# A mixer's softmax: probabilities scaled by 1/z on GpSimd ahead of their transposes, nine low parts of weights formed by GpSimd, and a new order

## The chip, the cores and the metric

The kernel runs on one core of a Trainium2 chip. The metric is the device time of one execution in microseconds (us), taken as the median of a few runs. Lower is better.

## What is computed

One layer of an encoder, on x of 512 positions by 1024 channels, all in float32:

```python
x = x + 0.5 * swiglu(rms_norm(x, ffn1_norm), ...)          # D_FF = 2752
u = rms_norm(x, mix_norm) @ w_in                           # 512 | 8x64 q | 2x64 k | 2x64 v
f_out = fourier_mixer(u[..., :512], fnet_w, fnet_b)        # Re(FFT2) per group of 128, then a linear map
a_out = gqa_attention(q, k, v, q_norm, k_norm)             # 8 query heads, 2 key heads, 512 x 512 scores
    p = jax.nn.softmax(scores, axis=-1); o = p @ v
x = x + concat([f_out, a_out]) @ w_out
x = x + 0.5 * swiglu(rms_norm(x, ffn2_norm), ...)
y = rms_norm(x, final_norm)
```

The change is in the attention of the middle part, in how the division by the softmax's sum z is done.

## The kernel before

**Numbers in two parts.** Every matrix operand is kept as a high part, rounded to the type fp32r that TensorE multiplies quickly, and a low part, the rest. A product takes three matmuls (high x high, high x low, low x high; `product`, L179). The high part of a weight is a cast, mostly on ACT; the low part is a subtraction, `lows` (L126), on VectorE.

**Stages.** First the feed-forward part (`ffn`, 0 to 330.9 us of the span), then the mixer (330.9 to 486.6), then the second feed-forward part with the final norm. The mixer works on 512 positions in eight banks of PSUM.

**The mixer's order.** Each step of the mixer is a named function in `ops`. The string `ORDER` (L47) lists all names; they are emitted in that order (L1314), and each of the five engines (PE, DVE, Activation, Pool, SP) then runs its own instructions strictly in the order of emission. Banks, buffers and slots are given out in that order too. So an instruction that waits on an engine holds up everything behind it on that engine.

**The names.** In names of the form `s`t`b`c, t is one of four pairs of query heads, b one of two key heads, c a block of 128 positions.

- `wX.r`, `wX.h`, `wX.l` (L799 to L817), and the same for `f0` to `f3`, `fw`, `o0` to `o7`: load a weight by a DMA from SP's queue into one of three `raw` buffers, cast its high part (ACT; VectorE for `f0` and `f1`), form its low part (VectorE). The two parts take a pair of slots out of three pairs in the mixer, so a high part waits until TensorE is through with the weight three back. A raw buffer is free when the low part is done.
- `k.0` to `k.7`, `q0.0` ..., `v.0` ...: the projections, one product each (L825). `.sq`, `.sw`, `.sd`, `.rc`, `.rs`, `.pq`, `.s0`, `.s1` (L838 to L900): squares, swapped halves by four small DMAs on SP's queue (`.sd`), rotation, and the norm of a head, whose power of -1/2 is on GpSimd (`.s1`, L900; `n1.p` is another, L255). `.ah`, `.al`, `.bh`, `.bl`: the parts of q.
- `f00.0` ... (L1003): Fourier projections; `map0`, `d00` ..., `c0.c` ...: the rest of the Fourier mixer. `pos` (L1310): three DMAs of its tables, issued by GpSimd.
- `s` (L1139): scores, two matmuls into a bank. `m` (L1146): on VectorE the maximum over a row (L1148) and a multiplication of 128x1 by the row's scale (L1149). `e` (L1152): the exponential on ACT, which also sums each row into `zs[t]`. The result, `prob[t, b, c]`, has queries on partitions and keys along them.
- `t` (L1164): four transposes of `prob` by TensorE, so that keys lie on partitions; each needs all four c of its t and b. `h` and `l` (L1171, L1177): high and low part of the transposed probabilities. `v` (L1206): values times probabilities, into `outs[t, b]`. `o..c`, `o..a` (L1218 to L1227) add the two halves of it into `pair[t]`.
- `z0.r`, `z0.w`, `z0.p` (L1186 to L1200): 1/z of all eight columns of a pair on VectorE, spread over 64 columns each by GpSimd, and turned into a row by four transposes on TensorE, into a bank. `r0.m` (L1231): the row multiplied into `pair[t]` on VectorE. `r0.h`, `r0.l`: its parts for the output projection.
- `y0.0` ... `y7.7` (L1242): the output projection; `.x`, `.h`, `.l`, `.q`, `.a`: residual, norm operands and squares.

So before, probabilities are left unscaled up to the very end, and 1/z is multiplied in once for each pair of heads.

Of the kernel before, what the change touches and what calls it, by code (L numbers as in the profile page):

```python
# [41 lines left out]
HI_DVE = ("f0", "f1")  # L42
SWAP_DMA = ("q1", "q2", "q3")
# [4 lines left out]
wq0.r wk.r wv.r wk.h pos wq0.h wk.l k.0 k.1 k.2 k.3 wq1.r k.4 wq1.h k.5 k.6 k.7 wv.h n1.c k.sq wq0.l q0.0  # L48
q0.1 q0.2 cos k.pq wq1.l n1.m q0.3 q0.4 k.sw f3.r q0.5 wv.l wq2.r k.s0 q0.6 k.s1 k.rc q0.7 q1.0 wq2.h k.rs
q1.1 q1.2 q1.3 q0.rc q0.sq kw f1.r wq2.l kp v.0 q0.sw km k0.2 q0.pq k0.0 k1.0 q0.s0 v.1 q1.4 q0.rs k1.3 q1.5  # L50
v.2 wq3.r k0.1 v.3 q0.bh q1.6 k0.3 q1.7 q2.0 q0.ah q1.sq q0.al s000 v.4 q0.bl v.5 wq3.h s001 s002 s003 q0.s1
v.6 k1.1 m000 k1.2 q1.sw wq3.l q1.sd q2.1 e000 m002 m003 q1.rc m001 q1.pq e002 v.7 q1.s0 q1.rs vt q3.0 s011
q1.s1 e001 q2.2 m011 vp q2.3 q1.ah q2.4 s010 f0.r f2.r q1.al q3.1 q2.5 q2.6 e003 q2.7 f0.h q3.2 n1.p m010
q2.sw s012 q3.3 f0.l f1.h t000 e010 q2.sd e011 q2.rc m012 t003 vs q2.sq h000 fw.r t001 s013 e012 s102 t002
f1.l m102 q3.4 v.h q3.5 h002 q3.6 f00.0 l000 s100 m013 h001 l002 v.l l001 e013 e102 q3.7 q2.pq f2.h m100 v000
q3.sw z0.r q3.sd t010 q2.s0 q1.bh q2.s1 v001 q2.rs f01.0 e100 f2.l s101 f00.1 q2.ah h010 m101 q3.sq f02.0
q1.bl l010 o2.r s103 v002 e101 f02.1 h003 t011 q3.rc q2.bh f00.u l003 h011 m103 q2.bl v003 t013 f02.e e103
t012 o0.r q3.rs q3.pq s112 v010 q3.ah l011 f01.1 q2.al s110 q3.s0 h012 h013 s113 l012 v011 o00.c o00.a l013
m113 m112 s212 e113 m110 f03.0 f01.u e112 m212 q3.al o1.r t103 f03.1 f3.h t101 h101 v012 q3.s1 h103 f03.e
l101 v013 e212 t100 h100 o01.c f10.0 f3.l l103 fw.h s213 l100 q3.bh f12.0 o01.a s111 f03.h f10.1 f02.h q3.bl  # L60
t102 f10.u f03.l e110 s210 s211 h102 v100 m213 z0.w e213 f02.l m111 v101 e111 s201 m210 m211 f12.1 o5.r l102
f12.e e211 z0.p r0.m t111 t112 v102 h111 h112 fw.l l112 v103 o10.c s203 f12.h e210 t110 f11.0 h110 m201 l111
o4.r m203 f13.0 o10.a t113 o0.h s202 t210 f12.l e203 l110 f11.1 v110 r0.h o0.l h113 s200 f11.u m202 f13.1
r0.l z1.r e201 map1 l113 t211 m200 v111 o1.h map1.h map0 f13.e d00 d01 h210 f13.h o1.l map1.l f13.l l210
map0.h v112 v113 e200 t213 d0.h h211 map0.l l211 s302 e202 s301 v210 t212 h213 h212 d0.l d10 z1.w m302 o11.c
d11 v211 e302 l213 t200 s300 d1.h l212 m301 d1.l h200 o11.a t201 c0.s v212 s311 m300 c0.c e301 m311 c0.q t203
e300 e311 h203 d20 v213 o21.c s303 d21 c0.o h201 l200 t202 v200 o3.r m303 s312 l203 c1.c z2.r e303 o21.a c1.s
d30 c0.h d2.h l201 c1.q z1.p t300 m312 v201 d2.l c1.o d31 c2.s h202 e312 r1.m s310 l202 s313 c2.q c1.h t301
d3.h c0.l m313 c2.c h300 v202 e313 c1.l v203 y0.0 o20.c m310 h301 l300 c2.o y0.1 e310 d3.l l301 o20.a z2.w
z3.r y1.0 y1.1 c2.h t303 v300 o2.h c3.s c3.c t310 v301 c3.q o7.r t302 c2.l y1.2 h310 h303 c3.o h302 y0.2 l302  # L70
t312 z2.p c3.h v302 c3.l t311 h311 l310 l303 y1.3 y1.4 o6.r z3.w r1.h l311 t313 v310 y0.3 h313 o2.l v303
o30.c r1.l y2.0 y1.5 v311 y2.1 h312 l313 l312 r2.m v312 v313 z3.p o30.a y2.2 y0.4 r2.h o31.c r2.l o31.a y1.6
y0.5 r3.m y0.6 r3.h y2.3 r3.l y0.7 y2.4 o3.h y2.5 y2.6 o3.l y1.7 y2.7 y1.x y3.0 o5.h o5.l y3.1 y3.2 y2.x y0.x
y3.3 y2.q o4.h y5.0 y3.4 o4.l y3.5 y5.1 y0.q y1.q y3.6 y5.2 y5.3 y3.7 y5.4 y5.5 y4.0 y5.6 y4.1 y3.x y4.2 o6.h
y1.h y4.3 y2.h y5.7 y4.4 o6.l y4.5 o7.h y5.x y0.h y6.0 y5.h y4.6 y3.h y1.l y1.a o7.l y3.q y6.1 y2.l y5.q y4.7
y7.0 y4.x y4.q y3.l y7.1 y6.2 y2.a y7.2 y4.h y6.3 y5.l y6.4 y6.5 y3.a y0.l y7.3 y6.6 y6.7 y4.a y5.a y7.4 y6.x
y4.l y7.5 y6.h y6.l y6.q y7.6 y7.7 y7.x y6.a y7.q y7.h y7.a y7.l
# [3 lines left out]
def asf(ap):  # L81
    return ap.bitcast(F32)
# [3 lines left out]
def encoder(ctx, tc, A, out):  # L86
# [39 lines left out]
    def lows(lo, src, hi):  # L126
        nc.vector.tensor_tensor(out=lo, in0=src, in1=asf(hi), op=ALU.subtract)  # L127
# [619 lines left out]
    with tc.tile_pool(name="mix", bufs=1) as mp, tc.tile_pool(name="mixt", bufs=1) as mt:  # L747
# [51 lines left out]
        def weight_ops(name, src, n=KD):  # L799
# [14 lines left out]
            @op(f"{name}.l")  # L814
            def _():
                hi, lo = ws[name]
                lows(lo[:, :n, :], raws[name][:, :n, :], hi[:, :n, :])  # L817
# [314 lines left out]
        prob, parts, pts, outs, pair, zs, zps, sps, mxs = {}, {}, {}, {}, {}, {}, {}, {}, {}  # L1132
# [50 lines left out]
        def sum_ops(t):  # L1183


            @op(f"z{t}.r")  # L1186
            def _():
                nc.vector.reciprocal(zs[t], zs[t])

            @op(f"z{t}.w")  # L1190
            def _():
                zw = tp.tile([P, 4, 2, HD], F32, tag="wide", bufs=1, name=f"zw{t}")
                nc.gpsimd.tensor_copy(zw, zs[t].unsqueeze(3).to_broadcast([P, 4, 2, HD]))
                zs[t] = zw
# [353 lines left out]
```

## Time and profile before

| | us |
|---|---|
| median of three runs | 826.18 |
| the three runs | 824.57, 826.18, 826.47 |
| span of the profiled execution, first to last instruction | 821.1 |
| the mixer within it | 330.9 to 486.6 |
| median less span | 5.1 |

The profile is of one execution, which is shown by its span; the median is of other executions and holds also what lies around the span. Granted clock of TensorE: 1.000. In the rows of the profile, PE is TensorE's matmuls, PEld its loads of the stationary operand, DVE VectorE, ACT ScalarE, POOL GpSimd, SP the queue that issues most DMAs. A row of a group gives line, engine, operation, out<-in with shapes, count, busy us, mean ns of one, and the engine's idle time just before; a row of the timeline begins with start and length in us. `mix` is any of the mixer's banks in PSUM. Matmuls overlap, so their length is more than the distance from one start to the next.

### The profile page before, as it was taken

Reading aid. Unit: us, or ns where it says so; the run is one execution under the profiler, and the core shown is the slowest. Engines: PE = TensorE matmul, PEld = TensorE weight load, DVE = VectorE, ACT = ScalarE, POOL = GpSimd, SP = SyncE. Lnnn points to the kernel's source line nnn. Section 1 sums busy time; section 2 is a strip of 40 time slices with the busy share of each in tenths; the row PEclk is TensorE's granted clock in tenths of the full one; section 3 lists DMA queues with packets and bytes.
Section 4 is the critical chain, followed back from the end, with each engine's and each line's share of the span. In section 5 each row is a group of like instructions: output and inputs, shape, how many; then the busy total and the mean of one; then the engine's idle time right before and its main releaser. Section 6 shows DMA issues by size and latency. Waiting matters only on the chain.

```text
span 821.1 us, 13621 instructions
## 1 busy us (share of the span) xinstructions
PE 814.0 (99%) x5378; PEld 747.0 (91%) x5378; DVE 640.8 (78%) x996; ACT 464.5 (57%) x777; POOL 30.6 (4%) x34
## 2 busy tenths in 40 slices
PE   9999999999999999999999999999999999999997
PEld 7889999899989998889998888899989999899986
DVE  7998896489756947799998488998945896479574
ACT  7764664167524635676886358556632673256462
POOL 0110000000000000222000000100000000000001
PEclk9999999999999999999999999999999999999999
DMA  7664322323242213621110233552232322322222
GB/s 257 182 145 174 123 91 78 123 103 141 66 153 89 74 58 116 225 77 52 52 52 27 87 105 105 123 170 112 93 121 112 126 103 69 131 104 97 69 78 103
DMA packets 31168, 89.58 MB, mean 109 GB/s; under 512 B 3712, under 2 KB 8832, under 8 KB 31104
## 3 DMA queue, kind: packets, MB, share of 16 engines
q1 hardware_dynamic: 27776, 82.61, 28.9%
q0 software_dynamic: 2608, 5.12, 3.3%
q10 hardware_dynamic: 720, 0.98, 0.3%
q8 instruction: 42, 0.69, 0.3%
q14 instruction: 22, 0.18, 0.1%
HBM read 84.24 MB, written 2.10 MB: 105 GB/s over the span
## 4 chain that ended last, share of the span: by engine, by line
PE 97%; DVE 1%; issue 1%; DMA 0%; ACT 0%; POOLq 0%; POOL 0%; DVEq 0%
PE dn L183 25%; PE r L419 23%; PE q L419 12%; PE mix L183 9%; PE gu L183 8%; PE p L419 6%; PE gu L708 3%; PE mix L1211 2%; PE mix L1168 2%; PE mix L1142 1%; PE mix L1006 1%; PE mix L1008 1%; PE mix L1007 1%; PE mix L1143 1%; PE mix L1065 1%
## 5 line engine op out<-in xcount | busy, mean ns | idle before, releaser
L419 PE MATMUL r<-rt,ring 128*128 128x256 f32 x1686 | 209.3, 276 | 0.0
L183 PE MATMUL dn<-at,ring 128*128 128x512 f32 x900 | 203.3, 380 | 0.5 <-DVE ring L127 0.4
L419 PEld LDWEIGHTS r<-rt,ring 128*128 128x128 f32 x1686 | 200.4, 188 | 0.8
L183 PEld LDWEIGHTS dn<-at,ring 128*128 128x128 f32 x900 | 168.1, 188 | 29.8 <-DVE ring L127 1.6
L419 PE MATMUL q<-rt,ring 128*128 128x256 f32 x840 | 106.6, 276 | 0.0
L127 DVE TENSOR_TENSOR ring<-s,ring 128x1024 fp32r<-128x1024 f32 x70 | 85.6, 1223 | 24.0 <-ACT ring L378 20.8
L419 PEld LDWEIGHTS q<-rt,ring 128*128 128x128 f32 x840 | 100.4, 188 | 0.0
L543 DVE SCALAR_TENSOR_TENSOR gx<-dn,gx 128x512 f32<-128x512 f32 x61 | 42.0, 690 | 67.6 <-PE dn L183 67.6
L378 ACT CAST ring<-s 128x1024 fp32r<-128x1024 f32 x70 | 73.5, 1050 | 28.0 <-PE p L419 13.6
L169 ACT CAST ring<-raw_dn 128x768 fp32r<-128x768 f32 (+3 forms) x58 | 45.2, 783 | 71.1 <-PE dn L183 62.2
L127 DVE TENSOR_TENSOR ring<-raw_dn,ring 128x768 fp32r<-128x768 f32 (+3 forms) x58 | 51.6, 893 | 5.7 <-PE r L419 4.4
L419 PE MATMUL p<-rt,ring 128*128 128x256 f32 x420 | 53.3, 276 | 0.0
L127 DVE TENSOR_TENSOR ring<-raw_g,ring 128x1024 fp32r<-128x1024 f32 x35 | 42.8, 1221 | 11.1 <-PE p L419 10.2
L419 PEld LDWEIGHTS p<-rt,ring 128*128 128x128 f32 x420 | 50.2, 188 | 0.0
L183 PE MATMUL gu<-ring 128*128 128x512 f32 x216 | 48.9, 381 | 0.0
L183 PEld LDWEIGHTS gu<-ring 128*128 128x128 f32 x216 | 40.4, 188 | 6.9
L378 ACT CAST ring<-raw_g 128x1024 fp32r<-128x1024 f32 x35 | 36.8, 1051 | 15.8 <-DMA raw_g<-in_wgu 8.5
L427 ACT COPY p<-r 128x256 f32<-128x256 f32 x35 | 13.0, 371 | 46.8 <-PE r L419 46.5
L451 ACT ACTIVATE g<-g 128x512 f32<-128x512 f32 x35 | 22.1, 633 | 23.4 <-DVE g L450 23.1
L387 ACT CAST ring<-raw_u 128x512 fp32r<-128x512 f32 x35 | 21.8, 624 | 17.4 <-PE q L419 15.9
L183 PE MATMUL mix<-near,ring 128*128 128x512 f32 x120 | 29.7, 383 | 0.0
L464 DVE TENSOR_TENSOR u<-g,u 128x512 f32<-128x512 f32 x35 | 24.1, 689 | 6.1 <-ACT u L463 6.0
(269 smaller groups left out, 1300.5 us busy)
## 6 DMA issues: line engine op xcount, KB each, us to landing
raw_g<-in_wgu SPq DMA_DIRECT2D x35, 512.0 KB, 3.6
raw_u<-in_wgu SPq DMA_DIRECT2D x35, 512.0 KB, 4.4
raw_dn<-in_wd SPq DMA_DIRECT2D x40, 384.0 KB, 3.1
raw_gu<-in_wgu SPq DMA_DIRECT2D x12, 512.0 KB, 3.7
raw_o<-in_wo SPq DMA_DIRECT2D x8, 512.0 KB, 3.5
raw_dn<-in_wd SPq DMA_DIRECT2D x8, 448.0 KB, 3.4
raw_wq<-in_wins SPq DMA_DIRECT2D x4, 512.0 KB, 3.6
raw_f<-in_winf SPq DMA_DIRECT2D x4, 512.0 KB, 4.5
```

What stands on the lines that cost most here:

```text
L127: nc.vector.tensor_tensor(out=lo, in0=src, in1=asf(hi), op=ALU.subtract)
L169: nc.scalar.copy(hi[:, :n, :], raw[:, :n, :])
L183: nc.tensor.matmul(ps, a, b, start=first and b is mhi and a is whi, stop=last and a is wlo)
L378: nc.scalar.copy(hi, src)
L387: nc.scalar.copy(hi, src)
L419: nc.tensor.matmul(ps[:, t], a[:, ks], b[:, i, t], start=first and i == 0 and o == 0, stop=i == KH - 1 and o == 2, skip_group_check=not first,
L451: nc.scalar.activation(b["g"], b["g"], AF.Silu)
L464: nc.vector.tensor_tensor(out=u, in0=b["g"], in1=u, op=ALU.mult)
L543: nc.vector.scalar_tensor_tensor(out=x[d][:, t], in0=ps[:, t], scalar=0.5, in1=x[d][:, t], op0=ALU.mult, op1=ALU.add)
L708: nc.tensor.matmul(turned(pss[c]), w[:, k % 2, c], turned(m[k]), start=k == 0 and m is hh and w is hi, stop=k == KD - 1 and w is lo,)
L1168: nc.tensor.transpose(pts[n][:, c * P : (c + 1) * P], prob[t, b, c][:, kc * P : (kc + 1) * P], ident)
L1211: nc.tensor.matmul(turned(outs[t, b]), w, turned(p), start=kc == 0 and i == 0, stop=kc == 3 and i == 1)
```

## The change

- `z{t}.r`, `.w`, `.p` and `r{t}.m` go: no spread copy, no sixteen transposes, no four multiplications, and the bank for the row goes with them.
- `z{t}{b}` takes the reciprocal of one half of `zs[t]` (eight of them, where there were four of the whole).
- `p{t}{b}{c}` multiplies each of the 32 tiles of probabilities by its column of 1/z, in place, on GpSimd, between `e` and `t`.
- The low parts of `wq1`, `wq2`, `wq3`, `wv`, `f0` to `f3` and `fw` are formed by GpSimd; `wk`, `wq0` and `o0` to `o7` stay on VectorE.
- `ORDER` is new throughout: all five engines run their mixer steps in another order. Only its beginning, and a piece with the first head's `z` and `p`, are shown.

```diff
+LOWS_POOL = ('wq1', 'wq2', 'wq3', 'wv', 'f0', 'f1', 'f2', 'f3', 'fw')
...
-wq0.r wk.r wv.r wk.h pos wq0.h wk.l k.0 k.1 k.2 k.3 wq1.r k.4 wq1.h k.5 k.6 k.7 wv.h n1.c k.sq wq0.l q0.0
...
+wk.r wk.h wk.l wq1.r wq0.r k.0 k.1 k.2 k.3 k.4 wv.r k.5 wq0.h k.6 n1.c cos wq0.l q0.0 q0.1 k.7 wq1.h wv.h q0.2
+q0.3 wq3.r k.sq q0.4 q0.5 n1.m k.pq wq1.l k.s0 q0.6 wv.l q0.7 v.0 v.1 q1.0 q1.1 q1.2 k.sw wq2.r k.rc q0.sw k.s1
...
+vt s011 q1.ah q2.sq f0.h q1.pq q1.s0 s012 m003 q2.sw q3.1 q3.2 n1.p s013 m011 e010 e000 q3.3 q1.al e003 f0.l
+m013 q1.s1 q1.bh vp f1.h z00 e013 q3.4 m012 s101 q1.bl f2.r e011 q2.pq q3.5 p000 f00.0 m101 p001 vs s103 o2.r
+p002 m103 q2.rc e012 q2.sd q3.6 q3.7 z01 p003 f1.l q2.rs e101 f3.r t002 v.h q3.sq q3.sw q2.s0 t003 p010 f2.h
...
-    def lows(lo, src, hi):
-        nc.vector.tensor_tensor(out=lo, in0=src, in1=asf(hi), op=ALU.subtract)
+    def lows(lo, src, hi, by=nc.vector):
+        by.tensor_tensor(out=lo, in0=src, in1=asf(hi), op=ALU.subtract)
...
-                lows(lo[:, :n, :], raws[name][:, :n, :], hi[:, :n, :])
+                lows(lo[:, :n, :], raws[name][:, :n, :], hi[:, :n, :], nc.gpsimd if name in LOWS_POOL else nc.vector)
...
-            @op(f"z{t}.r")
-            def _():
-                nc.vector.reciprocal(zs[t], zs[t])
-
-            @op(f"z{t}.w")
-            def _():
-                zw = tp.tile([P, 4, 2, HD], F32, tag="wide", bufs=1, name=f"zw{t}")
-                nc.gpsimd.tensor_copy(zw, zs[t].unsqueeze(3).to_broadcast([P, 4, 2, HD]))
-                zs[t] = zw
-
-            @op(f"z{t}.p")
-            def _():
-                zps[t] = bank_for(f"z{t}")
+            for b in range(2):
+
+                @op(f"z{t}{b}")
+                def _(b=b):
+                    nc.vector.reciprocal(zs[t][:, :, b], zs[t][:, :, b])
+
                 for c in range(4):
-                    nc.tensor.transpose(zps[t][:, c * P : (c + 1) * P], zs[t][:, c].rearrange("p a b -> p (a b)"), ident)
+
+                    @op(f"p{t}{b}{c}")
+                    def _(b=b, c=c):
+                        e = prob[t, b, c]
+                        nc.gpsimd.tensor_scalar(out=e, in0=e, scalar1=zs[t][:, c, b : b + 1], scalar2=None, op0=ALU.mult)
...
-            @op(f"r{t}.m")
-            def _():
-                nc.vector.tensor_tensor(out=pair[t], in0=zps[t], in1=pair[t], op=ALU.mult)
-                read(f"z{t}")
-
```

More of the change, by code (lines that the diff above doesn't have):

```diff
@@ L47 @@
 ORDER = """
-wq0.r wk.r wv.r wk.h pos wq0.h wk.l k.0 k.1 k.2 k.3 wq1.r k.4 wq1.h k.5 k.6 k.7 wv.h n1.c k.sq wq0.l q0.0
[L49 to L62, printed above, removed]
@@ L68 @@
[L68 to L72, printed above, removed]
```

37 lines of the change are left out of this document (26 added, 11 removed).

## The prediction

> **What bounds the kernel now.** I read the page first, for the engine that ends the span, then the stretch of the mixer in five windows, then the waits inside it, then the chain. The first two lines are the page's head, the third its chain of work.
>
> ```profile
> span 821.1 us, 13621 instructions
> PE 814.0 (99%) x5378; PEld 747.0 (91%) x5378; DVE 640.8 (78%) x996; ACT 464.5 (57%) x777; POOL 30.6 (4%) x34
> ...
> PE 97%; DVE 1%; issue 1%; DMA 0%; ACT 0%; POOLq 0%; POOL 0%; DVEq 0%
> ```
>
> The chain is 97% TensorE, so only TensorE's own work or an idle gap on it can change the time. The mixer is the stretch from 330.9 to 486.6. Columns: stretch, then busy us of PE, PEld, DVE, ACT, POOL.
>
> ```profile
> 360.00:390.00 30.00, 30.00 (x200) 27.22 (x198) 28.87 (x53) 19.60 (x40) 7.03 (x5) 1.00 0.20 63
> 390.00:420.00 30.00, 30.00 (x216) 27.81 (x215) 28.96 (x56) 25.68 (x53) 0.62 (x1) 1.00 0.19 71
> 420.00:452.00 32.00, 32.00 (x203) 28.53 (x201) 28.64 (x60) 23.33 (x48) 1.23 (x2) 1.00 0.06 18
> 452.00:486.60 34.60, 34.60 (x159) 29.53 (x158) 22.14 (x29) 15.80 (x23) 0.00 (x0) 1.00 0.28 92
> ```
>
> TensorE is busy in all of it, at granted clock 1.00. VectorE is a close second: 86.5 of the 92 us from 360 to 452, so 5.5 us spare. GpSimd is nearly empty. A busy PE may hide waits, so I looked for TensorE among the waits of this stretch; there is one row:
>
> ```profile
> PEld mix L1142 <- DVE near L127: 0.4, 1, 0.4
> ```
>
> To see that no more is hidden, I added up TensorE's work by its spacings (start to start). Rows, the last from the chain:
>
> ```profile
> 379.63 0.38 PE L1142 MATMUL mix<-ks,near 128*128 128x512 f32 x1
> ...
> 380.08 0.38 PE L1211 MATMUL mix<-ph,near 128*128 128x512 f32 x1
> ...
> 380.52 0.28 PE L1006 MATMUL mix<-ring 128*128 128x256 f32 x1
> ...
> 381.91 0.60 PE L1168 MATMUL mix<-ident,e 128*128 128x128 f32 x4
> ...
> 415.44 0.87 PE L1065 MATMUL mix<-pos,near 128*128 128x258 f32 x6
> 416.16 0.62 PE L1065 MATMUL mix<-both,near 128*128 128x512 f32 x2
> ...
> 417.08 0.39 PE L1211 MATMUL mix<-ph,near 128*128 128x512 f32 x1
> ...
> 431.00 0.60 PE L1200 MATMUL mix<-ident,zw 128*128 128x128 f32 x4
> 431.43 0.60 PE L1168 MATMUL mix<-ident,e 128*128 128x128 f32 x4
> 431.79 0.47 PE L1211 MATMUL mix<-ph,near 128*128 128x512 f32 x1
> 432.10 0.38 PE L1211 MATMUL mix<-pl,near 128*128 128x512 f32 x1
> ```
>
> ```profile
> 452.22 34.37 PE mix L183 x156
> ```
>
> A score (s) or attended (v) step takes 0.445 us, half a Fourier projection (f) 1.38, the two halves of d 0.72 and 0.92, a product of three matmuls 3 x 34.37/156 = 0.66, a map step about as much, a c step a quarter of an f. Four transposes take 0.36 and make what follows 0.08 late: 431.79 to 432.10 is 0.31 where a plain matmul of 512 takes 0.22. Laid end to end from 330.92 in the old order, these make 485.5; the chain's products end at 452.22 + 34.37 = 486.6. So about 1.1 us in 156 is spacing that I can't name, and the floor of this stretch is TensorE's own work. Nothing taken off VectorE shortens the kernel by itself.
>
> **The change, part by part.** Rows by group (count, busy us, mean ns):
>
> ```profile
> L1200 PE MATMUL mix<-ident,zw 128*128 128x128 f32 x16 | 2.4, 272 | 0.0
> ...
> L1193 POOL COPY zw<-z 128x512 f32<-128x512 f32 x4 | 2.5, 613 | 54.0 <-PE mix L1200 30.8 <-ACT fu L1018 23.2
> ...
> L1232 DVE TENSOR_TENSOR oo<-mix,oo 128x512 f32<-128x512 f32 x4 | 2.7, 684 | 0.1
> ...
> L1188 DVE RECIPROCAL z<-z 128x8 f32<-128x8 f32 x4 | 0.8, 192 | 0.0
> ...
> L127 DVE TENSOR_TENSOR ring<-raw_f,ring 128x1024 fp32r<-128x1024 f32 x3 | 3.7, 1218 | 0.0
> ...
> L1334 POOL TENSOR_TENSOR gx<-gx,rb 128x256 f32<-128x256 f32 x2 | 1.4, 733 | 1.5 <-ACT rb L268 1.5
> ...
> L900 POOL TENSOR_TENSOR sc<-sc,mhalf 128x8 f32<-128x8 f32 x5 | 9.6, 1914 | 44.5 <-DVE sc L896 44.5
> ...
> L1312 POOL DMA_DIRECT2D pos<-in_pos x1 | 0.6, 577 | 0.0
> ...
> L812 ACT CAST ring<-raw_wv 128x1024 fp32r<-128x1024 f32 x1 | 1.0, 1047 | 2.2 <-issue 2.2
> ...
> L1156 ACT ACTIVATE e<-mix,mx,sc 128x512 f32<-128x512 f32 x32 | 25.0, 782 | 5.0 <-DVE mx L1149 4.8
> ...
> L812 DVE CAST ring<-raw_f 128x1024 fp32r<-128x1024 f32 x2 | 1.4, 690 | 0.0
> ...
> L1148 DVE TENSOR_REDUCE mx<-mix 128x1 f32<-128x512 f32 x32 | 21.9, 684 | 0.3 <-PE mix L1143 0.2
> ...
> L1149 DVE TENSOR_TENSOR mx<-mx,sc 128x1 f32<-128x1 f32 x32 | 5.1, 160 | 1.3
> ```
>
> *Removed.* Sixteen transposes of 1/z leave TensorE in four groups. A group costs 431.43 - 431.00 = 0.43 to 0.36 + 0.08 = 0.44: 4 x 0.44 = 1.76 us off the path. This is the only term that can shorten the kernel. The lay of the new order agrees: 483.7 instead of 485.5. Four copies on GpSimd and four multiplications on VectorE (4 x 0.68) go too, both beside TensorE: nothing on the path by themselves.
>
> *Moved.* Nine low parts go from VectorE to GpSimd: eight of 128x1024 at 1.22 and fw at 0.68 (half the length, as the row of 128x512 above), 10.4 us less on VectorE. With the multiplications gone and four more reciprocals (+0.8), VectorE is 12.4 us lighter. On GpSimd a low part isn't in the trace. Bounds: not below VectorE's 1.22; above four times the 128x256 row, 2.93. I take 2.5, near the upper end, since that row is the same operation on the same engine and only its fixed part is counted four times.
>
> *Added.* 32 multiplications of 128x512 by a column, p. Bounds: the copy of the same size with one input, 0.61; twice the two-input 128x256, 1.47. I take 0.65, nearest to the copy, as p too streams one tensor. GpSimd then has 32 x 0.65 + 8 x 2.5 + 1.3 = 42 us more, little beside 156. But its queue is in order, and four p stand between the last exponential of a head and the first transpose of its probabilities, which the old order did not have.
>
> By the Trainium skill, GPSIMD Engine Reference, section 3.1 (Elementwise), a two-input instruction takes about 2.6 cycles an element; a 128x1024 low part is then estimated at 1024 x 2.6 / 1.2 GHz = 2.2 us, and its one-input 512 elements at 0.77 us. No row here has either form; with 0.77 in place of 0.65 the sum below would be up to 0.5 later at each tight place.
>
> *Where a wait is added.* I placed the steps by the lay of the new order and looked at what TensorE would find. Names are of the order.
> - Start: wv.l waits for wv.h, which needs the slot that k.7 leaves at 338.0; one ACT cast (1.05) and 2.5 on GpSimd give 341.7, v.0 comes at 342.4. wq2.h is ACT's fifth step from there and starts near 346, so wq2.l ends near 349.6; q2.0 comes at 350.7. Covered by 0.7 and 1.1 us; at 2.93 and with a longer queue this cover goes and v.0 stalls a few tenths.
> - SP: a raw buffer is free only when its low part is done, so f0.r now waits for wq3.l on GpSimd, behind three DMA issues of pos (0.6 each), moved there, and q0.s1 (1.9). That ends near 357; f0.r is due near 359 behind q1's four swap DMAs. Covered.
> - **Tight place one, t002 at 371.5.** f0.r lands 4.5 later (row below), near 364; f0.h (0.69), q1.s0, m003 on VectorE, e003 on ACT, q1.al, m013 and z00 follow one by one: z00 ends near 368.6. GpSimd runs f0.l to 366.8 and q1.s1 to 368.6. Four p: 368.7 + 2.6 = 371.3. No margin.
> - **Two, t111 at 401.2.** e113 starts near 397.4, z11 is done at 398.7, four p end at 401.3.
> - **Three, t200 at 419.1**, behind z20 at 416.5: 419.2. **Four, t310 at 442.55**, behind e310 and z31 at 437.8: 440.4, covered by 2.
> - The other four heads have 2 to 12 us between z and the first transpose.
>
> ```profile
> raw_f<-in_winf SPq DMA_DIRECT2D x4, 512.0 KB, 4.5
> ```
>
> Behind a waiting p stand the next low part or q.s1 on GpSimd; behind a waiting transpose stands all of TensorE. Small overruns at places one to three, with the handover between engines, I put at 0.2 each: 0.6 us. **Sum:** -1.76 + 0.6 = -1.2, a span of 819.9. The span lies 5.1 us under the median of the three runs (826.18), and I carry that over: **825.0**.
>
> **Rivals.**
>
> *A. VectorE and GpSimd hold each other up (slower).* VectorE's instructions with two inputs in SBUF may share a way into SBUF with GpSimd. Rows, first of POOL, then of DVE:
>
> ```profile
> 340.10 1.68 POOL L900 TENSOR_TENSOR sc<-sc,mhalf 128x8 f32<-128x8 f32 x1 [7.18 <-DVE sc L896]
> 347.62 2.02 POOL L900 TENSOR_TENSOR sc<-sc,mhalf 128x8 f32<-128x8 f32 x1 [5.85 <-DVE sc L896]
> ```
>
> ```profile
> 341.08 0.68 DVE L877 TENSOR_TENSOR sw_k<-sw_k,sin 128x512 f32<-128x512 f32 x1
> ...
> 347.46 0.68 DVE L877 TENSOR_TENSOR sw_q<-sw_q,sin 128x512 f32<-128x512 f32 x1
> 348.18 0.69 DVE L878 TENSOR_TENSOR rot_q<-rot_q,sw_q 128x512 f32<-128x512 f32 x1
> ```
>
> At 347.62 GpSimd's instruction started under a two-input VectorE instruction and took 0.34 longer than at 340.10. VectorE's, on the other hand, took 0.68 and 0.69 while GpSimd's ran: no delay, but GpSimd read only 8 elements there. By the Trainium skill, SBUF — State Buffer, section Who interferes with whom, a two-input VectorE instruction and a GpSimd instruction that reads SBUF exclude each other for the whole instruction; the longer GpSimd row agrees, the unhindered VectorE rows don't.
>
> The price, if VectorE waits too. From 360 to 452 it has about 60 two-input instructions (the second half of each m, the lows of q, fe, fo and o, the rotations). GpSimd runs p for 32 x 0.65 = 21 of the 92 us and low parts or powers for some 13; meeting one in mid-run costs half of it: 60 x (0.23 x 0.33 + 0.14 x 1.25) = 15 us. VectorE's spare is 5.5 + 6.8 (four f lows and fw less, three multiplications, less 0.8 for the reciprocals) = 12.3. It decides from that point: 2.7 over, plus about 0.5 at each of four tight places: +4.7 on the forecast, **829.7**.
>
> *B. p is slow (slower).* At 1.3 us, four p take 2.6 more: places one, two and three late by 2.4, 2.8 and 2.7, place four by 0.5: 826.18 - 1.76 + 8.4 = **832.8**. It decides from about 0.9. Against it: the copy's 0.61.
>
> *C. All hidden, and the unnamed 1.1 us goes too (faster):* 826.18 - 2.86 = **823.3**. The old order stands against it: it was already laid without gaps.
>
> *D. The floor moves but nothing more:* -1.76 exactly, **824.4**; counted with the forecast.
>
> **How the numbers follow.** Forecast with D 0.50, A 0.27, B 0.13, C 0.10. Differences within 0.3% (2.5 us) are about what a measurement of this kernel can tell from no change; the forecast lies inside. The forecast's own range is 823.9 to 827.5 (low parts at 2.93, p at 0.8). A and B reach 829 to 833, C 823.3. The range that leaves out 2 in 10 is 823.3 to 831.5. Faster takes C and a little of the forecast: 0.12. Slower takes B, nearly all of A, and nothing else: 0.36. Same: 0.52.
>
> **What would show it.** Right: no zw transposes, the mixer's products ending near 485.4 instead of 486.6, TensorE waits of some tenths before transposes t002, t111 and t200, and p near 0.65 us. A: VectorE's second instructions of m longer than 0.16 or VectorE rows of 0.68 grown, GpSimd's of one form with a wide spread, TensorE waiting for pl, mx or own results of VectorE. B: p with a mean above 0.9 and the waits named after POOL. I am wrong altogether if TensorE stalls at the weights (wv, f0, f2) by several us, or if a DMA that now starts later ends last.

## The result, and the profile after

| | us |
|---|---|
| before, median of 4 runs | 826.33 (824.57 to 827.99) |
| after, median of 4 runs | **846.03** (845.92 to 847.33) |
| ratio after to before, with 95% interval | **1.0247** (1.0225 to 1.0269): slower by 20 us |
| forecast | 825.0, range 823.3 to 831.5 |
| profiled execution of after: its time, its span | 845.92, 844.1 |

The forecast missed, and its range too. By the spans of the two profiled executions the change costs 844.1 - 821.1 = 23.0 us, by the ratio 20.4: before's profiled execution was shorter than its median. Costs within a trace are compared with 23.0 below, costs between kernels by ratios, each to before on the same chip; 0.1% is 0.83 us.

The page of after, head and chain:

```profile
span 844.1 us, 13640 instructions
PE 819.5 (97%) x5362; PEld 749.3 (89%) x5362; DVE 642.2 (76%) x987; ACT 464.2 (55%) x777; POOL 98.5 (12%) x71
...
PE 87%; DVE 5%; POOL 3%; issue 2%; ACT 1%; DMA 1%; SPq 0%; POOLq 0%; DVEq 0%; ACTq 0%
```

TensorE has its sixteen transposes less (5378 to 5362), but its share of the chain fell from 97% to 87%: it now waits. The stretches of the mixer (busy us of PE, PEld, DVE, ACT, POOL, then granted clock) show where:

```profile
360.00:390.00 30.00, 26.35 (x166) 23.19 (x166) 26.66 (x46) 18.35 (x37) 20.72 (x13) 1.00 0.29 93
390.00:420.00 30.00, 24.26 (x160) 21.57 (x158) 24.71 (x48) 19.43 (x41) 20.82 (x13) 0.94 0.10 29
420.00:452.00 32.00, 29.48 (x199) 26.68 (x198) 27.57 (x55) 23.85 (x48) 17.67 (x12) 1.00 0.15 49
```

Before, TensorE was busy for all of the 92 us. Now 12 are missing, and in the second stretch the clock is lower too. GpSimd has 59 us of work there where 9 stood before, though I had counted 42 more in the whole mixer. What TensorE waited for from 330 to 512 (total us, times, longest):

```profile
PEld mix L1169 <- POOL e L1198: 11.1, 8, 2.6
PEld mix L1143 <- ACT e L1157: 3.1, 1, 3.1
PEld mix L1143 <- ACT ks L954: 2.4, 1, 2.4
PEld gu L184 <- DVE ring L214: 1.7, 1, 1.7
PEld mix L1143 <- ACT near L921: 1.4, 1, 1.4
PEld mix L1291 <- issue: 1.4, 1, 1.4
PEld ss L242 <- issue: 0.4, 1, 0.4
```

Before, this list had one row of 0.4. These are 21.5 us, half of it transposes that wait for p (L1198). Two short stretches at a lower granted clock add the rest:

```profile
390.00:405.00 15.00, 12.14 (x76) 10.88 (x75) 13.00 (x25) 8.99 (x18) 9.78 (x6) 0.89 0.18 54
511.00:540.00 29.00, 29.00 (x130) 24.44 (x130) 24.97 (x42) 20.46 (x27) 4.57 (x4) 0.94 0.38 98
```

They cost 15 x 0.11 + 29 x 0.06 = 3.4 us. 21.5 + 3.4 - 1.76 (the transposes) = 23.1, against 23.0 measured. So waits and clock account for the loss, though that they do so to 0.1 is luck: these are the waits of the weight loads (PEld), while the matmuls themselves stood idle for 17.3 of the 182 us, and the transposes alone will measure 2.9 below. What remains is which part of the change makes which wait.

The GpSimd groups of after (count, busy us, mean ns):

```profile
L1198 POOL TENSOR_SCALAR e<-e,z 128x512 f32<-128x512 f32 x32 | 51.4, 1622 | 25.0 <-DVE z L1191 22.7 <-DMA sw_q<-own_q 2.3
...
L128 POOL TENSOR_TENSOR ring<-raw_f,ring 128x1024 fp32r<-128x1024 f32 x3 | 7.1, 2370 | 11.3 <-PE mix L890 6.9 <-ACT ring L813 4.5
```

A p takes 1.62 us, where I took 0.65 and gave 1.47 as the upper bound; four take 6.2 to 7.1 us between the last exponential and the first transpose. A low part takes 2.37, near the 2.5 that I took. And VectorE's own rows have changed, in a form that nobody edited (VectorE groups from 330 to 512):

```profile
L1150 DVE TENSOR_TENSOR mx<-mx,sc 128x1 f32<-128x1 f32 x32 | 7.9, 247 | 1.4
...
L879 DVE TENSOR_TENSOR rot_q<-rot_q,sw_q 128x512 f32<-128x512 f32 x4 | 5.6, 1389 | 0.1
...
L897 DVE TENSOR_TENSOR sc<-sc,eps_ms 128x8 f32<-128x8 f32 x5 | 4.3, 865 | 0.2
```

Before, L1150 (there L1149) took 160 ns, as the prediction shows, and the other two read:

```profile
L878 DVE TENSOR_TENSOR rot_q<-rot_q,sw_q 128x512 f32<-128x512 f32 x4 | 2.8, 692 | 0.1
...
L896 DVE TENSOR_TENSOR sc<-sc,eps_ms 128x8 f32<-128x8 f32 x5 | 0.8, 169 | 0.2
```

One of them in the timeline of after (start, length in us), GpSimd first, then VectorE:

```profile
348.43 2.46 POOL L128 TENSOR_TENSOR ring<-raw_wq,ring 128x1024 fp32r<-128x1024 f32 x1 [3.29 <-ACT ring L813]
```

```profile
347.98 0.68 DVE L878 TENSOR_TENSOR sw_q<-sw_q,sin 128x512 f32<-128x512 f32 x1
348.70 2.74 DVE L879 TENSOR_TENSOR rot_q<-rot_q,sw_q 128x512 f32<-128x512 f32 x1
```

The low part of wq2 runs from 348.43 to 350.89. VectorE's two-input instruction, due to start at 348.70, ends at 351.44: 350.89 and some 0.55 more, so it did most of its work after GpSimd had ended. While p runs, the picture is another:

```profile
401.32 6.20 POOL L1198 TENSOR_SCALAR e<-e,z 128x512 f32<-128x512 f32 x4 [0.77 <-DVE z L1191]
```

```profile
403.74 0.16 DVE L1150 TENSOR_TENSOR mx<-mx,sc 128x1 f32<-128x1 f32 x1
403.82 0.68 DVE L128 TENSOR_TENSOR near<-fe,near 128x512 fp32r<-128x512 f32 x1
```

Two-input instructions of VectorE took 0.16 and 0.68 in the middle of four p, their undisturbed times.

Theory: three things cost time by themselves: the length of p in the chain e, z, p, t (rival B, larger); the two-input low parts on GpSimd, which hold VectorE up (rival A, but from the low parts); and the new order. Rivals to it: p alone accounts for all of it; VectorE is held up by p; or the order alone lost the time.

### The profile page after: what moved, and what is told of

The parts are those of the page before. It is cut to its first block, busy times and chain, and to the rows that moved or that the text cites. A ratio compares the mean times of both kernels' runs of the same rounds, so it can differ in the third digit from the quotient of the medians.

```text
span 844.1 us, 13640 instructions
## 1 busy us (share of the span) xinstructions
PE 819.5 (97%) x5362; PEld 749.3 (89%) x5362; DVE 642.2 (76%) x987; ACT 464.2 (55%) x777; POOL 98.5 (12%) x71
## 4 chain that ended last, share of the span: by engine, by line
PE 87%; DVE 5%; POOL 3%; issue 2%; ACT 1%; DMA 1%; SPq 0%; POOLq 0%; DVEq 0%; ACTq 0%
PE dn L184 25%; PE r L420 23%; PE q L420 11%; PE gu L184 7%; PE p L420 6%; PE mix L184 5%; POOL e L1198 3%; PE gu L709 3%; PE mix L1209 1%; DVE mx L1149 1%; PE mix L1169 1%; PE mix L1066 1%; PE mix L1143 1%; DVE near L128 1%; PE mix L1144 0%
## 5 line engine op out<-in xcount | busy, mean ns | idle before, releaser
L1198 POOL TENSOR_SCALAR e<-e,z 128x512 f32<-128x512 f32 x32 | 51.4, 1622 | 25.0 <-DVE z L1191 22.7
L184 PE MATMUL gu<-ring 128*128 128x512 f32 x216 | 50.6, 390 | 1.3 <-DVE ring L214 1.3
L128 DVE TENSOR_TENSOR ring<-raw_g,ring 128x1024 fp32r<-128x1024 f32 x35 | 42.7, 1221 | 10.8 <-PE p L420 10.2
L256 POOL TENSOR_TENSOR r<-ms,mhalf 128x4 f32<-128x4 f32 (+1 forms) x4 | 4.7, 1180 | 363.3 <-DVE ms L249 363.3
L379 ACT CAST ring<-raw_g 128x1024 fp32r<-128x1024 f32 x35 | 36.8, 1051 | 16.6 <-DMA raw_g<-in_wgu 10.8
L128 POOL TENSOR_TENSOR more<-raw_wq,more 128x1024 fp32r<-128x1024 f32 x2 | 4.9, 2452 | 285.3 <-ACT more L813 285.3
L452 ACT ACTIVATE g<-g 128x512 f32<-128x512 f32 x35 | 22.2, 633 | 23.4 <-DVE g L451 23.1
```

Source lines behind the costliest of these rows:

```text
L128: by.tensor_tensor(out=lo, in0=src, in1=asf(hi), op=ALU.subtract)
L184: nc.tensor.matmul(ps, a, b, start=first and b is mhi and a is whi, stop=last and a is wlo)
L379: nc.scalar.copy(hi, src)
L452: nc.scalar.activation(b["g"], b["g"], AF.Silu)
L1198: nc.gpsimd.tensor_scalar(out=e, in0=e, scalar1=zs[t][:, c, b : b + 1], scalar2=None, op0=ALU.mult)
```

## The experiments

### The length of p, and the low parts: what each costs in the new order

All of these start from the changed kernel. First p, then the place of the low parts, then both.

**p as a copy, waiting for nothing.**

```diff
-                        nc.gpsimd.tensor_scalar(out=e, in0=e, scalar1=zs[t][:, c, b : b + 1], scalar2=None, op0=ALU.mult)
+                        nc.gpsimd.tensor_copy(e, e)
```

> The changed kernel with each p a plain copy of the tile onto itself on GpSimd, so that 1/z is left out. The copy of this size took 0.61 us before; p takes 1.57. Theory 1 (the time went to p's length): the waits of the first transposes for p (11.1 us) go and with them one of the two stretches of lower clock: 831 to 834. Theory 2 (the low parts on GpSimd hold up VectorE, and that is the larger part): 838 or more. Theory 3 (the new order is at fault, whatever the engines do): 844 or more.

Measured: 836.42, 1.0137 (1.0122 to 1.0152). The copy took 0.73 in the mean. Not quite half of the loss is gone, and the time lies between the ranges of theories 1 and 2; so p alone doesn't account for it.

**p with two inputs.**

```diff
+                        nc.gpsimd.tensor_tensor(out=e, in0=e, in1=zs[t][:, c, b : b + 1].to_broadcast([P, S]), op=ALU.mult)
```

> The changed kernel with p as a two-input multiplication, the second input the column of 1/z spread over the row. By fw's low part of the same size it should take 1.27 us instead of 1.57. Theory 1 alone: four p are 1.2 us shorter ahead of each of eight heads, so 837 to 841. Theory 2 in its sharper form (a two-input GpSimd instruction holds up VectorE's two-input ones, a one-input instruction doesn't): VectorE is now held up by p as well, its 0.16 us multiplications of m grow to a mean above 0.3, and the time stays at 844 or goes above.

Measured: 840.78, 1.0194 (1.0177 to 1.0211). The group of p on GpSimd:

```profile
L1198 POOL TENSOR_TENSOR e<-e,z 128x512 f32<-128x512 f32 x32 | 36.2, 1162 | 31.1 <-DVE z L1191 28.9 <-DMA sw_q<-own_q 2.3
```

The two-input product is shorter than the one-input one (1.16 against 1.62), but L1150 on VectorE grew to 322 ns from 247, a first sign that a two-input p holds VectorE up. The time stands in the range of p's length alone.

**The low parts back on VectorE.**

```diff
-LOWS_POOL = ('wq1', 'wq2', 'wq3', 'wv', 'f0', 'f1', 'f2', 'f3', 'fw')
+LOWS_POOL = ()
```

> The changed kernel with the nine low parts back on VectorE, the order unchanged. Theory 1: VectorE gets 10.4 us of work back, little is won, 842 to 847. Theory 2: the waits at the start (5.2 us in three places), the one for an exponential (3.1 us) and a stretch of lower clock go: 835 to 838. Theory 3: 845.

Measured: 843.87, 1.0232 (1.0201 to 1.0264). L879 fell to 764 ns and L897 to 210, near before's, yet the time hardly moved, as theory 1 had it: the wait for p grew instead. Taken by itself this run would clear the low parts; the table further down shows why that misleads. TensorE's waits, first row:

```profile
PEld mix L1169 <- POOL e L1198: 13.7, 9, 3.1
```

**Neither: the new order alone**, with p a `pass` and `LOWS_POOL = ()`.

```diff
-LOWS_POOL = ('wq1', 'wq2', 'wq3', 'wv', 'f0', 'f1', 'f2', 'f3', 'fw')
+LOWS_POOL = ()
...
-                        nc.gpsimd.tensor_scalar(out=e, in0=e, scalar1=zs[t][:, c, b : b + 1], scalar2=None, op0=ALU.mult)
+                        pass
```

> The changed kernel with no p at all (1/z is left out) and the low parts on VectorE: the new order and the removed transposes and multiplications alone. Theories 1 and 2: all that costs is gone, the 1.8 us of the sixteen transposes remain: 824 to 826. Theory 3: the order itself stalls TensorE, 830 or more.

Measured: 827.58, 1.0034 (1.0022 to 1.0045), between what theories 1 and 2 and what theory 3 expected. TensorE's three longest waits from 330 to 512:

```profile
PEld gu L184 <- DVE ring L214: 1.7, 1, 1.7
PEld mix L1143 <- ACT e L1157: 1.4, 1, 1.4
PEld mix L184 <- DVE ring L128: 0.7, 1, 0.7
```

The first row stands in after as well, at the mixer's end. So the order has losses of its own.

**The low parts alone**: p a `pass`, the nine low parts on GpSimd.

```diff
-                        nc.gpsimd.tensor_scalar(out=e, in0=e, scalar1=zs[t][:, c, b : b + 1], scalar2=None, op0=ALU.mult)
+                        pass
```

> The changed kernel with no p (1/z is left out) and the nine low parts on GpSimd: the fourth corner beside the changed kernel (844.9 at this chip's level), the one with the low parts on VectorE (843.9) and the one with neither (827.6). If the two costs simply add up, the low parts are worth 1 us and this gives 828 to 830. If each hides much of the other (TensorE waits for whichever is later), the low parts alone cost 5 to 8 us through VectorE's two-input instructions being held up: 832 to 836, near the 836.4 with p as a copy.

Measured: 833.34, 1.0095 (1.0082 to 1.0108): 0.61% or 5.0 us above the order alone, with no p at all. Three of TensorE's waits, and the VectorE group:

```profile
PEld mix L1143 <- ACT ks L954: 2.8, 1, 2.8
...
PEld mix L1143 <- ACT near L921: 1.4, 1, 1.4
PEld mix L1291 <- issue: 1.4, 1, 1.4
```

```profile
L879 DVE TENSOR_TENSOR rot_q<-rot_q,sw_q 128x512 f32<-128x512 f32 x4 | 4.8, 1205 | 0.1
```

These three waits stand in after too. They are in no list of a kernel of this order with the low parts on VectorE. VectorE's hold-up comes with the low parts, not with the one-input p.

**The low parts in the old order**: the kernel before, with the same nine on GpSimd.

```diff
+LOWS_POOL = ('wq1', 'wq2', 'wq3', 'wv', 'f0', 'f1', 'f2', 'f3', 'fw')
...
-                lows(lo[:, :n, :], raws[name][:, :n, :], hi[:, :n, :])
+                lows(lo[:, :n, :], raws[name][:, :n, :], hi[:, :n, :], nc.gpsimd if name in LOWS_POOL else nc.vector)
```

> The kernel before, with its own order, and only the nine low parts moved to GpSimd. Theory 2 (GpSimd's two-input low part holds up VectorE's two-input instructions wherever it stands): VectorE rows of 0.69 grow to 2 us and more in several places, 828 to 835. If the hold-ups hurt only through the places that the new order gives the low parts: 824 to 827.

Measured: 829.95, 1.0059 (1.0042 to 1.0075). The low parts cost 4.9 us there as well, so it isn't the new order that makes them dear.

**p by a constant**, in a single run, to see whether the column makes it slow.

```diff
+                        nc.gpsimd.tensor_scalar(out=e, in0=e, scalar1=0.5, scalar2=None, op0=ALU.mult)
```

> The changed kernel with p as the same one-input instruction, times 0.5 in place of the column of 1/z (so 1/z is left out). If the operand column makes p long: 0.6 to 0.8 us each and 836 or less. If a one-input instruction with arithmetic is long by itself: 1.5 us each, and 840 to 846.

Measured: 838.11 (one run, before on that chip 825.09). The group:

```profile
L1198 POOL TENSOR_SCALAR e<-e 128x512 f32<-128x512 f32 x32 | 51.3, 1623 | 12.4 <-ACT e L1157 11.3 <-issue 1.1
```

The same 1.62 without a column: it is the one-input multiplication on GpSimd that takes so long, not the fetch of the scalar. The run says more. Its p is as long as the change's, yet it is 1.6% above before and not 2.5%, less than was expected of a long p. It lacks the wait for 1/z, so a p can run as soon as its own exponential is done, and of the eight waits for p one is left:

```profile
PEld mix L1169 <- POOL e L1198: 1.1, 1, 1.1
```

So p's length costs most where four of them stand in a row behind 1/z (one run, so the size is rough).

### The forecast's price, and a 4-byte tile

To ask whether the price of p was the only failing step, p had to cost what the forecast said and still wait for 1/z. The first try had the first p of each head preceded by a copy of the column into a small new tile:

```diff
+                        if c == min(range(4), key=lambda k: PLACE.index(f"p{t}{b}{k}")):
+                            nc.gpsimd.tensor_copy(tp.tile([P, 1], F32, tag="zz", bufs=2, name=f"zz{t}{b}"), zs[t][:, c, b : b + 1])
+                        nc.gpsimd.tensor_copy(e, e)
```

> The changed kernel with each p a plain copy onto itself that still waits for the head's reciprocals (a copy of one column of them stands ahead of the first p of a head on GpSimd; the multiplication by 1/z is left out). So p costs the 0.61 to 0.65 us that the prediction took, all else as changed. If p's price was the only step that failed: 825 to 827. If the low parts that hold up VectorE cost about as much without p as with it, and p at this price adds a little: 835 to 838.

The same with `LOWS_POOL = ()`:

> The same, with the low parts on VectorE: p at 0.61 us after the reciprocals, nothing that holds up VectorE (1/z is left out). No p at all gave 827.6, p at 1.57 gave 843.9. If the waits of the first transposes grow with four times p's length beyond the room of the order (about 2.5 us): 828 to 831. If any p in the chain costs what p costs, whatever its length: 838 or more.

Measured: 862.13, 1.0445 (1.0429 to 1.046), and 857.49, 1.0393 (1.0376 to 1.041). Both missed their ranges, by 24 us and more, and in a place that the edit doesn't touch. Matmuls of the feed-forward stages in the second of them (count, busy us, mean ns), then the same groups before:

```profile
L423 PE MATMUL r<-rt,ring 128*128 128x256 f32 x1686 | 220.1, 283 | 0.0
L187 PE MATMUL dn<-at,ring 128*128 128x512 f32 x900 | 209.9, 390 | 0.0
```

```profile
L419 PE MATMUL r<-rt,ring 128*128 128x256 f32 x1686 | 209.3, 276 | 0.0
L183 PE MATMUL dn<-at,ring 128*128 128x512 f32 x900 | 203.3, 380 | 0.5 <-DVE ring L127 0.4
```

The products of these groups are longer by 7 to 10 ns, in stages that have no p. The suspect was the place of the tiles behind the new one in SBUF. So the same tile was put into the kernel before:

```diff
+                nc.gpsimd.tensor_copy(tp.tile([P, 1], F32, tag="zz", bufs=2, name=f"zz{t}"), zs[t][:, 0, 0:1])
                 zw = tp.tile([P, 4, 2, HD], F32, tag="wide", bufs=1, name=f"zw{t}")
```

> The kernel before, complete, with one tile of 4 bytes a partition (two buffers) added to the pool of temporaries, written once in each half of the mixer by a GpSimd copy of one element a partition that nobody reads. The work added is some 0.1 us on an engine that is idle there. If the 29 us that two kernels with such a tile lost against their expectation come from where the tile puts the others (all of the feed-forward products took 283 and 390 ns there, not 276 and 380), this kernel takes 850 to 856 us, and its products of 256 columns 283 ns. If they came from the copy of 1/z or from the wait, it takes 824 to 827 us.

Measured: 852.73, 1.0335 (1.0313 to 1.0356): 27.7 us for a tile that nobody reads.

```profile
L419 PE MATMUL r<-rt,ring 128*128 128x256 f32 x1686 | 220.1, 283 | 0.0
...
L183 PE MATMUL dn<-at,ring 128*128 128x512 f32 x900 | 210.4, 391 | 0.9 <-DVE ring L127 0.9
```

The tile alone, with its four tiny copies, makes the products longer; the two kernels above say nothing on p and are left aside. The question was asked again without a new tile, the column copied onto itself:

```diff
+                        if c == min(range(4), key=lambda k: PLACE.index(f"p{t}{b}{k}")):
+                            nc.gpsimd.tensor_copy(zs[t][:, c, b : b + 1], zs[t][:, c, b : b + 1])
+                        nc.gpsimd.tensor_copy(e, e)
```

> The changed kernel with p as a copy, and with p's wait for 1/z kept without any added tile: on GpSimd, ahead of the first p of each head in the order, the column of 1/z that this p would have used is copied onto itself. 1/z is left out of the result. The price is that of the forecast (0.61 to 0.73 us) and so are the low parts on GpSimd, the order and the wait. If the mis-sized p was the only step that failed, the time is that of the forecast, 824 to 827 us. By the theory that there were three failing steps (p, the low parts on GpSimd that hold VectorE up, the order's end), it is 835 to 839 us, as with the copy that waits for nothing (836.4).

The same with `LOWS_POOL = ()`:

> The same, with the nine low parts on VectorE (1/z left out of the result, p a copy that waits for 1/z, the new order). By the theory of three failing steps only the order's end is left of them: 828 to 831 us, near the order alone (827.6). If the wait for 1/z by itself costs something that the runs so far have hidden, 833 us or more.

Measured: 835.88, 1.0130 (1.0106 to 1.0153), and 830.18, 1.0056 (1.0038 to 1.0073). Both as the theory of three failing steps has it. The first kernel has the forecast's price of p and everything else of the change, and is still 10.7 us slower than before. TensorE's five longest waits in it:

```profile
PEld mix L1146 <- ACT ks L957: 2.4, 1, 2.4
PEld mix L1146 <- ACT e L1160: 1.8, 1, 1.8
PEld gu L187 <- DVE ring L217: 1.7, 1, 1.7
PEld mix L1146 <- ACT near L924: 1.4, 1, 1.4
PEld mix L1296 <- issue: 1.4, 1, 1.4
```

No transpose waits for p here, nor in the shorter waits (up to 0.7) behind these. What is left is mostly the low parts' waits (ks, near, issue), the order's (gu), and one for an exponential (1.8, where the order alone has 1.4).

**The two-input p with the low parts on VectorE**, a middle length, as a further point:

```diff
-LOWS_POOL = ('wq1', 'wq2', 'wq3', 'wv', 'f0', 'f1', 'f2', 'f3', 'fw')
+LOWS_POOL = ()
...
+                        nc.gpsimd.tensor_tensor(out=e, in0=e, in1=zs[t][:, c, b : b + 1].to_broadcast([P, S]), op=ALU.mult)
```

> A whole kernel: the changed one with the low parts on VectorE and p as a two-input multiplication, 1.0 us each where it runs undisturbed. Between the two others by length: a head's four take 4.0 us, 1.5 more than the order's room, against 3.8 more at 1.57. By length alone 833 to 837; with VectorE held up by p as well, 838 to 842.

Measured: 834.31, 1.0110 (1.0094 to 1.0125), with 4.5 us of waits for p: in the range of length alone. L1150 took 236 ns here, against 176 under the one-input p and 159 with no p, all three with the low parts on VectorE. So a two-input p does delay VectorE, though the time doesn't show it. Laid side by side:

| p | low parts on VectorE | low parts on GpSimd |
|---|---|---|
| none | 1.0034 | 1.0095 |
| copy, waits for 1/z | 1.0056 | 1.0130 |
| two inputs | 1.0110 | 1.0194 |
| one input times a column (the change) | 1.0232 | 1.0247 |

Down a column the time rises with p. Across a row the low parts cost 0.6 to 0.8%, save in the last. There, with the low parts back on VectorE, the waits for p grew from 11.1 to 13.7 us, and three stretches at half clock stood in the trace instead of two, some 1.7 us more. So the two costs overlap, and undoing one alone lets the other grow: that is why taking the low parts back gained only 0.15%.

### The gain, and the order

**The gain alone**: the kernel before without the spread, the sixteen transposes and the four multiplications, nothing put in their place.

```diff
-                zps[t] = bank_for(f"z{t}")
-                for c in range(4):
-                    nc.tensor.transpose(zps[t][:, c * P : (c + 1) * P], zs[t][:, c].rearrange("p a b -> p (a b)"), ident)
+                pass
...
-                nc.vector.tensor_tensor(out=pair[t], in0=zps[t], in1=pair[t], op=ALU.mult)
-                read(f"z{t}")
+                pass
```

> The kernel before with the rows of 1/z left out: no spread copies, no sixteen transposes, no four multiplications (so 1/z is left out), its own order otherwise. It measures the one gain of the prediction, 1.76 us. If that term was right: 1.5 to 2.0 us less than before, a ratio near 0.998. If TensorE gives the time back elsewhere: 1.000.

Measured: 822.39, 0.9965 (0.9953 to 0.9978), a gain of 2.9 us (1.8 to 3.9), more than the 1.5 to 2.0 expected. It is the only kernel of the study below before, and it isn't a whole one. Against it, the order alone, which also has neither rows nor p, stands 0.69% or 5.7 us (some 4.3 to 7.1) higher: that is the price of the order, with its four more reciprocals.

**The order's end**: the order alone, with its last products moved.

```diff
-y4.5 y7.0 y4.6 y7.1 y1.l y4.7 y6.4 y7.2 y5.h y5.q y7.3 y2.a y3.h y5.l y3.q y4.x y7.4 y4.q y0.l y3.a y4.h y7.5
-y6.5 y6.6 y6.7 y3.l y6.x y4.a y7.6 y6.h y6.q y4.l y5.a y7.7 y7.x y6.a y6.l y7.h y7.q y7.a y7.l
+y4.5 y7.0 y4.6 y7.1 y1.l y4.7 y6.4 y6.5 y6.6 y6.7 y7.2 y5.h y5.q y7.3 y2.a y3.h y5.l y3.q y4.x y7.4 y4.q y0.l
+y3.a y4.h y6.x y7.5 y6.h y3.l y4.a y7.6 y6.q y4.l y5.a y7.7 y7.x y6.a y6.l y7.h y7.q y7.a y7.l
```

> The order alone once more (no p, so 1/z is left out; low parts on VectorE), with the last three products of y6 and their followers two products earlier, as late as they stood in the old order. Theory: what the new order costs by itself is mostly its end, where VectorE is late with the operands of the next part by 1.3 us and TensorE's clock then drops to half for 3.4 us: 3 us less than the 827.6 of the order alone, 824 to 825. If the end isn't it: 827 to 828.

Measured: 825.66, 1.0008 (0.9997 to 1.0018): 0.26% or 2.1 us less than the order alone where 3 were expected, and the wait of gu for L214 is gone from the list. Of the order's 5.7 us this is the part that is settled; the rest stands in single waits of 0.2 to 1.4 us for VectorE's and ACT's results, which were not taken apart.

### Ways to keep the change

**The multiplication of m by a column**, in the old order with the low parts on GpSimd, so that it reads one tensor only:

```diff
-                nc.vector.tensor_tensor(out=mx, in0=mx, in1=f, op=ALU.mult)
+                nc.vector.tensor_scalar(out=mx, in0=mx, scalar1=f, scalar2=None, op0=ALU.mult)
```

> The kernel before with the nine low parts on GpSimd, as in the run that gave 829.95, and the second instruction of each m as a multiplication by a column (one tensor input and a scalar operand) instead of a product of two tensors. There its mean had gone from 160 to 350 ns. If only an instruction with two tensor inputs in SBUF is held up: the mean is back at 160 to 180 ns and the time at 826 to 828. If a column operand is held up as well: 300 ns and more, and 829 to 831.

Measured: 827.85, 1.0042 (1.0027 to 1.0057), against 1.0059 without it: the intervals overlap, so a gain in time isn't shown. The rows of m fell to 214 ns from 350. Not to before's 160, but all 32 of them lie between 212 and 216, where the two-input form had gone up to 1980: this form is longer by itself, and is not held up at all.

**p shared among three engines and among two**, the low parts on VectorE, the moved end:

```diff
+                        e, col = prob[t, b, c], zs[t][:, c, b : b + 1]
+                        at = sorted(range(4), key=lambda k: PLACE.index(f"p{t}{b}{k}")).index(c)
+                        by = ('POOL', 'ACT', 'DVE', 'ACT')[at]
+                        if by == "ACT":
+                            nc.scalar.activation(e, e, AF.Copy, scale=col)
+                        else:
+                            (nc.gpsimd if by == "POOL" else nc.vector).tensor_scalar(
+                                out=e, in0=e, scalar1=col, scalar2=None, op0=ALU.mult
+                            )
```

> A whole kernel: the new order with the end moved as in the run that gave 825.66, the low parts on VectorE, and the four p of a head on three engines: the first on GpSimd, the second and fourth on ACT, the third on VectorE. The slowest share is then one GpSimd instruction of 1.55 us, less than the 2.5 us for which the order has room, where four of them took 6.2. If p's length ahead of the first transposes was what the low parts on VectorE left of the loss (843.9): 825 to 829. If VectorE or ACT become too full: above 830.

and with `('ACT', 'DVE', 'ACT', 'DVE')`:

> As the three-engine kernel, but with the four p of a head on ACT and VectorE, two each, and none on GpSimd. About 1.3 us for a head's four. If GpSimd's 1.55 us was the last to end: 0 to 2 us less than with three engines. If VectorE's load counts (8 more instructions of 0.4 us): 1 to 3 us more.

Measured: 833.39, 1.0103 (1.0089 to 1.0117), and 832.23, 1.0086 (1.0073 to 1.01). Both better than the change, both worse than before, and the first above the 825 to 829 hoped for. A p took 0.73 on ACT and 0.50 on VectorE, but neither engine has the room: the waits are now for `e` from ACT (4.1 us in the first) and from VectorE (3.6 in the second). No whole kernel of the study beats before.

## Why the prediction was wrong, point by point

- **The bound** (TensorE's own work, VectorE second): right. Every loss found is an idle gap of TensorE or its clock.
- **The gain of 1.76 us:** real. Alone it measures 2.9 (1.8 to 3.9), nearer to rival C's 2.86, in which the unnamed 1.1 goes too; the interval hardly tells the two apart.
- **The low part on GpSimd, 2.5 us:** right, 2.35 to 2.46; fw 1.27 against 1.3.
- **p at 0.65 us: the term that failed most.** It is 1.62, 2.5 times the value taken, and its shortest (1.55) lies outside my upper bound of 1.47. The 0.77 named beside it was hardly nearer. I chose the copy as the nearest row since "p too streams one tensor"; the copy was the wrong kin. The other end, twice the two-input product, was wrong as a bound, since the one-input multiplication takes longer here than the two-input one. By the same places as in the prediction, four p at 1.62 come 4 x 0.97 = 3.9 later: 3.7, 4.1, 4.0 and 1.8 at places one to four, 13.6 in all. TensorE waited 3.0, 2.6, 3.2 and 1.4 there, and 0.9 at a fifth head, 11.1 in all. So the mechanism was rival B's, at the places that the prediction named, and the price was too low. From the copy that waits to the change is 1.17%, 9.7 us, with the low parts on GpSimd; 1.76%, 14.5 us, with them on VectorE.
- **VectorE's rows, taken as unchanged: failed.** The covers at the start held: TensorE waits for no low part that GpSimd formed. But VectorE's work beside them was late. That is rival A, in part. I weighed a short GpSimd instruction of 8 elements, under which VectorE wasn't hindered, against the rule that the prediction names, and let it count. Under a low part of 1024 elements VectorE is held for the whole of it. The rival counted only the stretch from 360; TensorE's first two such waits are ahead of it (at 336.7, 1.4, and at 359.8 for ks, 2.4), the third at 372 (near, 1.4). A third of the rival's 15 us stood on p, which with one input hardly hinders VectorE. The low parts cost 0.74%, 6.1 us, between the two kernels at the forecast's price, against 4.7 for the rival: near by luck, since the places were others.
- **The new order at nothing: failed.** I laid it by TensorE's work alone (483.7 against 485.5) and looked at the places where p and the weights are tight. What VectorE and ACT owe TensorE in it I didn't lay. It costs 5.7 us, 2.1 of them at the end.
- **Transfers:** right that none is late. f0.l ended at 369.8 instead of 366.8, but not for its load, which was issued at 360.2 and needs some 4: VectorE, busy without a break, came to the cast f0.h only at 366.5 to 367.2, and the low part began 0.2 later.
- **The clock:** not foreseen. I took gaps at their length; two of them cost some 1.7 us more each.

By ratios, step after step: rows gone -0.35%, order +0.69, p as a copy that waits +0.22, low parts on GpSimd +0.74, p's real price +1.17: 2.47%. Each has an uncertainty of 0.2 to 0.3, and the last two depend on the order in which they are added, since they act together. The wait for an exponential (3.1 us in after) shows how. Rows of after, GpSimd and VectorE:

```profile
389.76 2.35 POOL L128 TENSOR_TENSOR more<-raw_f,more 128x1024 fp32r<-128x1024 f32 x1
```

```profile
390.09 2.03 DVE L1150 TENSOR_TENSOR mx<-mx,sc 128x1 f32<-128x1 f32 x1
```

The exponential waited for an m that took 2.03 us instead of 0.16 and ended when the low part did. The low part stood there because four p had run just before it, from 382.65 to 389.79; with no p it ran at 382.12, and the wait was 0.7. With the low parts on VectorE the list has no such row. So some 1.9 of the 3.1 us needed both.

## What to carry to other kernels

Take the price of an instruction from a row of the same operation on the same engine; if there is none, a row of another operation isn't a bound, and a step that stands four times in a chain multiplies the error. A long instruction that may start early cost little here; the same one behind a common result, four in a row, was paid in full. Work that is moved to an idle engine isn't free if the two engines can't work at the same time: look at the busy engine's two-input rows, not at the idle engine's share. On a kernel that TensorE bounds, lay all engines' work in a new order, not TensorE's alone; a gap can also be paid in clock, as two were here.

## What the runs showed of the hardware

**Three prices on GpSimd for 128x512 in float32.** Medians of 32: copy 0.61, product with a spread column as the second input 1.04, one input times a constant 1.49, times a column 1.57. The one low part of this size, with two whole inputs, took 1.27. By the Trainium skill, GPSIMD Engine Reference, section 4.1 (Engine selection), two-input operations are the slow ones and one-input ones run at about line rate; here the one-input multiplication is the slower, and only the copy is fast.

**Who holds whom.** A low part on GpSimd, which has two inputs, held VectorE's two-input instruction for its whole length (2.74 us instead of 0.69), as the Trainium skill, SBUF — State Buffer, section Who interferes with whom, has it. The one-input p hardly did (rows of 0.16 and 0.68 under it; m 176 ns in the mean against 159 with no p), which that rule doesn't tell apart. On VectorE's side, m with one tensor input stayed at 212 to 216 ns beside the low parts.

**Half clock after a short gap, but not each time.** TensorE around the end of the mixer in after, first its matmuls, then stretches of 2 us (the clock is the third number from the right):

```profile
510.77 0.73 PE L184 MATMUL gu<-ring 128*128 128x512 f32 x2 [1.26 <-DVE ring L214]
511.47 1.25 PE L242 MATMUL ss<-ones,acc 128*128 128x2 f32 x8
```

```profile
510.00:512.00 2.00, 1.23 (x7) 0.86 (x8) 1.98 (x4) 0.00 (x0) 0.00 (x0) 1.00 0.95 317
512.00:514.00 2.00, 2.00 (x8) 1.72 (x8) 0.16 (x1) 0.18 (x1) 1.00 (x1) 0.53 0.39 152
514.00:516.00 2.00, 2.00 (x7) 1.63 (x6) 1.10 (x2) 1.97 (x3) 0.04 (x1) 0.62 0.00 0
516.00:518.00 2.00, 2.00 (x13) 1.68 (x12) 0.84 (x2) 1.67 (x3) 0.00 (x0) 1.00 0.35 76
```

An idle 1.26 us, with matmuls of 2 columns behind it, is followed by 3 to 4 us at about half clock: 1.7 us more on a gap of 1.3. The copy without a wait, the order alone, the change with its low parts on VectorE and the two kernels with the new tile show the same. But six other kernels have this gap, at the same place of the program and of the same length, and kept a clock of 1.00 behind it: the low parts alone, p by a constant, p with two inputs (both kernels) and the copy that waits without a new tile (both). So the gap's length alone doesn't decide it; what does was not found.

**The place of a tile.** Four bytes a partition, added to a pool, made the products of 256 columns in the feed-forward parts take 283 ns instead of 276 and the products `dn`, of 512 columns, 391 instead of 380. Three groups of 256 columns and the 900 products `dn` make 10.8 + 5.6 + 2.8 + 7.1 = 26.3 of the 27.7 us. Not every product grew: `gu`, whose row names `ring` alone as its operands, stayed at 381. That the tile does it is shown; that it does so by shifting addresses, and which operand's, was not tried.
